# State-space outputs on two column tiles and the chunk kernel's product turned round on four

## The chip, the core and the metric

The kernel runs on one core of a Trainium2 chip. The metric is the time of one execution on the device in microseconds (us), and the median over several runs is compared.

## What is computed

A trunk of two layers over 256 tokens of 2048 channels. Layer 0 has a spatial-gating mixer, layer 1 a state-space mixer; a convolutional gated feed-forward follows each. The change touches the state-space mixer and what is prepared for it: 128 heads, each with 16 input channels, 64 complex states and 16 output channels.

```python
bbar_r, bbar_i = _cmul(qr[..., None], qi[..., None], b_re, b_im)      # per head: 64 states x 16 channels
def chunk_step(carry, u_c):
    bur = einsum('gpc,btgc->btgp', bbar_r, u_c); bui = ...            # inputs into the states
    pr, pim, hr, hi = associative_scan(combine, (a_r, a_i, bur, bui)) # h[t] = abar * h[t-1] + bu[t]
    ...
    y = einsum('gcp,btgp->btgc', cr, hr) - einsum('gcp,btgp->btgc', ci, hi) + dd * u_c
...
ga, gb = split(gelu(y) @ w_glu, 2); out = ga * sigmoid(gb)
```

Everything is float32.

## The kernel before

All large products run with weights streamed from HBM in tiles of up to 1 MB. `Weights` splits each tile into a high part (`wh`, L115, ScalarE) and a low part (`wl`, L116, VectorE), and `form_a_steps` multiplies blocks of 128 output features by 256 tokens: L767 is `wh` with 512 moving columns, L768 is `wl` with 256, into the tile `acc`. These two lines alternate through most of the kernel.

The state-space mixer works on chunks of 4 tokens. Its operators are built by `s5_prep` as background work: small steps of it are put between the weight tiles of layer 0's feed-forward. One of its parts, in the pool "prep_k", builds the chunk kernel, which leads from a chunk's inputs to its outputs, for 16 groups of 8 heads. Each group multiplies `qg` (128 states by 80 columns, stationary) with `bri` (128 states by 16 columns, moving) once per head, 8 float32 matmuls on L445 into `ps_k`. Each float32 matmul stands in the trace as two passes, so there are 16 records. ScalarE copies the 80 x 128 result (L449, `kc`), TensorE transposes it (L452, `ps_kt`), then VectorE (L454) and ScalarE (L460) place it in `tt`, and POOL's queue writes it to DRAM (L461, `td`). `bri` itself is filled earlier by four ScalarE copies (L386) with 16 columns per head.

In layer 1, `S5Tokens` handles 16 blocks of 8 heads (128 channels). Per block: `send` writes inputs u to DRAM, `load` reads them back (`ubd`) with the operator `pw`, `load1` reads tables, `load2` reads `qw` and `tw`, all on SP's queue; `drive` multiplies into `ps_x` (L574); `take`, `scan` and `turn` run the recurrence on VectorE and ScalarE; `outputs` makes `ps_y`; `gelu` applies the activation (L641, ScalarE) to `y` and writes it to DRAM (L642, SP's queue, `yd`); `fetch` reads it back turned (L646, POOL's queue, `yt`); `finish` splits it into `Gt` (L782, L783) for the gated product. The table `N_OF` puts each step in a slot between weight tiles; a scheduler then fixes the order on each queue. ScalarE, VectorE, SP and POOL each run in order, so a waiting instruction holds what is queued behind it. `ps_x` and `ps_y` share two PSUM buffers.

`outputs` has two sets of float32 matmuls with 64 output rows: L628, four on 128 moving columns (chunk inputs through `tw`, the chunk kernel), and L633, eight on 64 moving columns (states through `qw`, one per head). All go to PSUM partitions 0 to 63, 512 columns in all. `y` has one buffer.

Of the kernel before, what the change touches and what calls it, by code (L numbers as in the profile page):

```python
# [17 lines left out]
P = 128  # L18
# [17 lines left out]
def bcast(ap2d, n, axis):  # L36
    """[p, m] -> [p, n, m] (axis 1) or [p, m, n] (axis 2), repeated without a copy."""
    p, m = ap2d.shape
    if axis == 1:
        return ap2d.rearrange("p (o m) -> p o m", o=1).to_broadcast([p, n, m])  # L40
    return ap2d.rearrange("p (m o) -> p m o", o=1).to_broadcast([p, m, n])


def rsqrt_newton(nc, v, y, t):
    """y = v ** -0.5 (float32, three Newton steps); t is scratch."""
    V = nc.vector
    V.tensor_scalar(y.bitcast(I32), v.bitcast(I32), -0.5, RSQ, ALU.mult, ALU.add)
    for _ in range(3):
        V.scalar_tensor_tensor(t, y, -0.5, y, ALU.mult, ALU.mult)
        V.tensor_tensor(t, t, v, op=ALU.mult)  # L50
        V.scalar_tensor_tensor(y, t, 1.5, y, ALU.add, ALU.mult)


def rsqrt_column(nc, v, y, t, w):
    """rsqrt_newton for v of one column; t and w are scratch."""
    V = nc.vector
    V.tensor_scalar(y.bitcast(I32), v.bitcast(I32), -0.5, RSQ, ALU.mult, ALU.add)
    V.tensor_scalar(w, v, -0.5, None, ALU.mult)
    for _ in range(3):
        V.scalar_tensor_tensor(t, y, w, y, ALU.mult, ALU.mult)  # L60
        V.scalar_tensor_tensor(y, t, 1.5, y, ALU.add, ALU.mult)


# Slot of each group of 8 state-space heads, and how many slots later its results are read back and gated.
N_OF = (3, 4, 6, 7, 8, 9, 10, 11, 12, 13, 14, 16, 18, 20, 22, 24)
LAT = (4, 6)
# Products on constants that raise the tensor engine's clock while the input arrives.
N_WARM = 7
# Background work after each weight tile of the projection, of the FFN's up and of its down products.
# [5 lines left out]
class Weights:  # L75
    """Streams weight tiles in order of use and splits each into a high and a low float32r part."""
# [63 lines left out]
def w_tiles(w2d, k_chunk0, nk_total, col_segs, kt):  # L140
    """Tiles of a weight matrix: all of its K chunks for the given column segments."""
    out, k = [], 0
    width = sum(n for _, n in col_segs)
    while k < nk_total:
        nk = min(kt, nk_total - k)
        r0 = (k_chunk0 + k) * P
        segs = [
            (w2d[r0 : r0 + nk * P, c0 : c0 + n].rearrange("(k p) c -> p k c", p=P), n)
            for c0, n in col_segs
        ]  # L150
        out.append((segs, nk, width))
        k += nk
    return out


def exp_poly(nc, tl, x, out):
    """out = exp(x) in float32, by range reduction; tl(name, dtype) makes scratch like x."""
# [24 lines left out]
def sincos_poly(nc, tl, x, cos, sin):  # L182
    """cos and sin of x in float32, by reduction to a quarter turn."""
# [44 lines left out]
def s5_prep(tc, psum, ident, io, scr, rho):  # L228
    """Builds the state-space operators for chunks of 4 tokens and writes them to DRAM scratch.

    pd[h][c][j][(ri p)]   chunk input  -> state:  abar^(3-j) * Bbar
    qd[(ri p)][h][80]     state -> output: C * abar^tau (16 c x tau 1..4), then C itself
    td[(h % 2, c, j)][h // 2][(c' j')]  chunk input -> output inside the chunk, with the skip d on its diagonal
    rd[g][(h // 64, p)][2][16 h][64]  cos and sin of 4 * theta * k, heads 16 g .. of each half
    rho[(2 p), h]         |abar| ** 4

    Yields the vector engine's microseconds of each step, or None where the next step needs this one done.
    """
# [5 lines left out]
    with ExitStack() as keep:  # L244
        kp = keep.enter_context(tc.tile_pool(name="prep", bufs=1))
        tm = kp.tile([P, 512], F32, name="tm")
        bri = kp.tile([P, NH, 16], F32, name="bri")
# [3 lines left out]
        with ExitStack() as inner:  # L251
# [128 lines left out]
            for g in range(4):  # L380
                ps = psum.tile([P, 512], F32, name=f"ps_bri{g}", tag="misc")
                for i in range(4):
                    nc.tensor.transpose(
                        ps[:, i * P : (i + 1) * P], bb[:, 4 * g + i].rearrange("h r p -> h (r p)"), ident
                    )
                A.copy(  # L386
                    bri[:, :, 4 * g : 4 * g + 4].rearrange("q h c -> q c h"), ps.rearrange("q (c h) -> q c h", c=4)
                )
                yield 1.0
# [31 lines left out]
        with tc.tile_pool(name="prep_k", bufs=1) as pool:  # L421
# [17 lines left out]
            for g in range(16):  # L439
# [4 lines left out]
                for i in range(8):  # L444
                    nc.tensor.matmul(  # L445
                        ps[:80, i * 16 : (i + 1) * 16], qg[:, i, :], bri[:, 8 * g + i, :], start=True, stop=True
                    )
                kc = pool.tile([80, P], F32, name=f"kc{g}", tag="kc", bufs=2)
                A.copy(kc, ps[:80, :P])  # L449
                yield None  # L450
                ps = psum.tile([P, 512], F32, name=f"ps_kt{g}", tag="misc")
                nc.tensor.transpose(ps[:, :80], kc, ident[:80, :80])  # L452
# [54 lines left out]
class S5Tokens:  # L507
    """The state-space mixer for 8 heads (one block of 128 channels) at a time, in chunks of 4 tokens."""
# [21 lines left out]
    def send(self, s):  # L530
        """The block's inputs, to be read back as [(head, channel, token of chunk), chunk]."""
        ud = self.scr[4]
        self.nc.sync.dma_start(dram(ud, s * 32768, [[256, P], [1, 256]]), self.u.pop(s).rearrange("p j k -> p (j k)"))

    def load(self, s):
        """What the states need."""
# [12 lines left out]
    def load1(self, s):  # L549
        """What the scan needs."""  # L550
# [8 lines left out]
    def load2(self, s):  # L559
        """What the outputs need."""  # L560
# [8 lines left out]
    def drive(self, s):  # L569
        """Chunk inputs into the state space."""  # L570
# [7 lines left out]
    def take(self, s):  # L578
        """Into a frame that turns with the phase of abar ** 4."""
# [22 lines left out]
    def turn(self, s):  # L602
        """Back to the fixed frame; sp[.., h, k] is the state before chunk k."""
# [18 lines left out]
    def outputs(self, s):  # L622
        """States before each chunk and its inputs to y."""
# [3 lines left out]
        for i in range(4):  # L627
            nc.tensor.matmul(  # L628
                ps[:64, i * P : (i + 1) * P], st["tw"][:, i, :], st["ubd"][:, i, :],
                start=i == 0, stop=False, skip_group_check=True,  # L630
            )
        for h in range(8):
            nc.tensor.matmul(  # L633
                ps[:64, h * 64 : (h + 1) * 64], st["qw"][:, h, :64], st["sp"][:, h, :],
                start=False, stop=h == 7, skip_group_check=True,
            )

    def gelu(self, s):
        st = self.st.pop(s)
        y = self.pool.tile([64, 8, 64], F32, name=f"y{s}", tag="y", bufs=1)  # L640
        self.nc.scalar.activation(y.rearrange("q h k -> q (h k)"), st["y"][:64, :], AF.Gelu_apprx_tanh)  # L641
        self.nc.sync.dma_start(dram(self.scr[5], s * 32768, [[64, 64], [4096, 8], [1, 64]]), y)  # L642
# [11 lines left out]
def tile_hybrid_trunk(  # L654
# [86 lines left out]
    def bg(budget):  # L741
        """Runs steps of the background work for about that many microseconds of the vector engine."""
# [9 lines left out]
    def form_a_steps(Xt, nks, blocks, evac, k0=0):  # L752
        """Blocks of 128 output features by 256 tokens, weights stationary; yields after each weight tile.

        nks: chunks per weight tile, the first k0; blocks: column offset of each block in the tile; evac(pair, psum) follows
        each pair's last product.
        """
# [16 lines left out]
    def form_a(Xt, nks, blocks, evac, after=None, k0=0):  # L774
        """form_a_steps, with after[i]() behind tile i."""
# [4 lines left out]
    def split_to(dst, src):  # L780
        """dst[:, :256], dst[:, 256:] = high and low float32r parts of src."""
# [3 lines left out]
    def stage_x(k, g_col, src=None):  # L785
        """X[k] = parts of h[:, k] (or src) * g."""
# [7 lines left out]
    def sumsq(tp, k):  # L794
        """Adds the squares of h[:, k] to sq."""
# [7 lines left out]
    def make_r(tp):  # L803
        """rbc[:, t] = rsqrt(mean over channels of h ** 2 + eps), on every partition."""
# [9 lines left out]
    def residual(tp, ps, k, g_col=None, perm=False):  # L814
        """h[:, k:k+2] += product in ps; with g_col also the next stage's X and sum of squares."""
# [8 lines left out]
    def sum_parts(tp, ps, scaled=True):  # L824
        """(main + correction) [* r] of a pair of blocks -> [P, 2, 256] in SBUF."""
# [57 lines left out]
    def fetch_conv(tp, l):  # L883
        """Convolution taps and biases: loaded, then (place_conv) turned to a column per block of 128 channels."""
# [15 lines left out]
    def form_b_steps(Xt, nks, pss, own=0, between=None):  # L900
        """128 tokens by 512 output features in each of two banks, activations stationary; yields after each chunk.

        The last `own` chunks are taken by the first 128 tokens, then, after between(), by the others.
        """
# [25 lines left out]
    def total_r(ss, v, r, t):  # L930
        """r[:, a] = rsqrt(sum of ss[:, a, :] / D + eps)."""
# [10 lines left out]
    with ExitStack() as sgu_ctx:  # L942
# [33 lines left out]
        def turn_x(i):  # L976
            """Chunks 2 i and 2 i + 1 of the input, turned to channels by tokens."""
# [132 lines left out]
    n_tmp[0] = 1  # L1110
    with tc.tile_pool(name="s5", bufs=1) as sp:
# [58 lines left out]
        def glu_keep(i0):  # L1170
            """Half of the sum of a gate and value pair waits in the place of X."""
# [122 lines left out]
```

## Time and profile before

| | |
|---|---|
| runs of the kernel before | 2149.72 us median of three (2145.82 to 2150.45) |
| span of the profiled execution, first to last instruction | 2150.8 us |
| time of the profiled execution as a run | not listed apart; its span is 1.1 us above the median |
| TensorE busy | 2117.9 us, 98% of the span |
| VectorE, ScalarE busy | 1605.7 us, 1127.2 us |

A row of a timeline has the start in us, the duration in us, engine, line, operation, tiles and count; records that follow each other on one line are merged, and what stands in brackets is the idle time before them and what ended it. A matmul's duration runs to the end of its pipeline, so consecutive matmuls overlap, and the distance of their starts is what each costs. "128*64 128x128" is 128 rows by 64 columns of weights, and 128 rows by 128 columns of moving data. PE is TensorE, DVE VectorE, ACT ScalarE, and SPq the queue of SyncE that issues transfers.

### The profile page before, as it was taken

Reading aid. Unit: us, or ns where it says so; the run is one execution under the profiler, and the core shown is the slowest. Engines: PE = TensorE matmul, PEld = TensorE weight load, DVE = VectorE, ACT = ScalarE, POOL = GpSimd, SP = SyncE. Lnnn points to the kernel's source line nnn. Section 1 sums busy time; section 2 is a strip of 40 time slices with the busy share of each in tenths; the row PEclk is TensorE's granted clock in tenths of the full one; section 3 lists DMA queues with packets and bytes.
Section 4 is the critical chain, followed back from the end, with each engine's and each line's share of the span. In section 5 each row is a group of like instructions: output and inputs, shape, how many; then the busy total and the mean of one; then the engine's idle time right before and its main releaser. Section 6 shows DMA issues by size and latency. Waiting matters only on the chain.

```text
span 2150.8 us, 31583 instructions
## 1 busy us (share of the span) xinstructions
PE 2117.9 (98%) x12023; PEld 1829.1 (85%) x12023; DVE 1605.7 (75%) x2455; ACT 1127.2 (52%) x1682; POOL 90.2 (4%) x141
## 2 busy tenths in 40 slices
PE   8999999999999999999999999999999999999998
PEld 7888888888878888888888788888888888888886
DVE  6576788997997655899878866987665777557675
ACT  6544446553455534555556555555543555445553
POOL 1010000000002111000000000000000000000000
PEclk9999999999999999999999999999999999999999
DMA  7665556667668665665799986565565555655553
GB/s 259 196 187 171 192 188 203 219 213 232 208 208 253 211 203 179 193 214 188 246 277 272 254 236 190 184 204 183 181 205 183 181 193 183 198 191 178 194 196 117
DMA packets 359303, 438.84 MB, mean 204 GB/s; under 512 B 31376, under 2 KB 275696, under 8 KB 358512
## 3 DMA queue, kind: packets, MB, share of 16 engines
q1 hardware_dynamic: 349696, 407.94, 60.3%
q0 software_dynamic: 9424, 28.88, 4.4%
q8 instruction: 94, 1.54, 0.3%
q14 instruction: 57, 0.47, 0.1%
q10 hardware_dynamic: 32, 0.01, 0.0%
HBM read 414.66 MB, written 22.02 MB: 203 GB/s over the span
## 4 chain that ended last, share of the span: by engine, by line
PE 88%; DMA 5%; DVE 4%; issue 1%; ACT 1%; SPq 0%; ACTq 0%; DVEq 0%
PE acc L767 47%; PE acc L768 24%; PE accb L911 4%; PE accb L910 4%; PE accb L912 4%; PE accv L911 1%; PE accv L912 1%; PE accv L910 1%; DMA yd<-y 1%; DVE wl L116 1%; DMA w<-in_b_w_glu_dram 1%; PE ps_k L445 1%; DMA vn<-in_x_dram 1%; DMA w<-in_b_w_in_dram 0%; PE ps_x L574 0%
## 5 line engine op out<-in xcount | busy, mean ns | idle before, releaser
L767 PE MATMUL acc<-X,wh 128*128 128x512 f32 x3328 | 1174.8, 398 | 1.3 <-DVE z L829 0.8
L116 DVE TENSOR_TENSOR wl<-w,wh 128x1024 fp32r<-128x1024 f32 (+1 forms) x721 | 867.3, 1219 | 394.7 <-ACT wh L115 390.2
L115 ACT CAST wh<-w 128x1024 fp32r<-128x1024 f32 (+1 forms) x721 | 735.9, 1047 | 707.2 <-PE acc L767 525.5
L768 PE MATMUL acc<-X,wl 128*128 128x256 f32 x3328 | 930.6, 281 | 2.5 <-DVE wl L116 2.5
L767 PEld LDWEIGHTS acc<-X,wh 128*128 128x128 f32 x3328 | 623.2, 188 | 148.5 <-DVE z L829 1.7
L768 PEld LDWEIGHTS acc<-X,wl 128*128 128x128 f32 x3328 | 628.3, 189 | 6.7 <-DVE wl L116 3.9
L767 PE MATMUL acc<-Gt,wh 128*128 128x512 f32 x1472 | 519.2, 398 | 0.8 <-DVE kept L1177 0.8
L768 PE MATMUL acc<-Gt,wl 128*128 128x256 f32 x1472 | 409.2, 281 | 0.0
L767 PEld LDWEIGHTS acc<-Gt,wh 128*128 128x128 f32 x1472 | 275.2, 188 | 64.6 <-DVE kept L1177 1.2
L768 PEld LDWEIGHTS acc<-Gt,wl 128*128 128x128 f32 x1472 | 278.0, 189 | 2.4
L910 PE MATMUL accb<-wh,Gt 128*128 128x512 f32 x352 | 136.8, 389 | 0.0
L912 PE MATMUL accb<-wh,Gt 128*128 128x512 f32 x352 | 136.8, 389 | 0.0
L911 PE MATMUL accb<-wl,Gt 128*128 128x512 f32 x352 | 136.8, 389 | 0.0
L845 ACT ACTIVATE a<-z,conv 128x256 f32<-128x256 f32 x176 | 96.2, 595 | 17.1 <-DVE z L831 16.9
L827 ACT COPY t<-acc 128x512 f32<-128x512 f32 x96 | 55.7, 580 | 75.0 <-PE acc L768 75.0
L829 DVE TENSOR_TENSOR z<-acc,t 128x512 f32<-128x512 f32 x96 | 65.8, 685 | 25.5 <-ACT t L827 25.3
L851 DVE SCALAR_TENSOR_TENSOR a<-z,conv,a 128x254 f32<-128x254 f32 x176 | 80.3, 475 | 0.0
L848 DVE SCALAR_TENSOR_TENSOR a<-z,conv,a 128x255 f32<-128x255 f32 x176 | 77.3, 476 | 1.0 <-ACT a L845 1.0
L910 PEld LDWEIGHTS accb<-wh,Gt 128*128 128x128 f32 x352 | 66.1, 188 | 13.9
L912 PEld LDWEIGHTS accb<-wh,Gt 128*128 128x128 f32 x352 | 66.1, 188 | 13.8
L911 PEld LDWEIGHTS accb<-wl,Gt 128*128 128x128 f32 x352 | 66.1, 188 | 13.5
L831 DVE TENSOR_TENSOR z<-z,rbc 128x512 f32<-128x512 f32 x96 | 65.8, 686 | 1.2
(303 smaller groups left out, 1394.7 us busy)
## 6 DMA issues: line engine op xcount, KB each, us to landing
w<-in_f_w_up_dram SPq DMA_DIRECT2D x352, 512.0 KB, 4.6
w<-in_f_w_down_dram SPq DMA_DIRECT2D x80, 1024.0 KB, 5.1
w<-in_a_w_in_dram SPq DMA_DIRECT2D x31, 1024.0 KB, 5.6
w<-in_b_w_glu_dram SPq DMA_DIRECT2D x62, 512.0 KB, 5.3
w<-in_a_w_out_dram SPq DMA_DIRECT2D x16, 1024.0 KB, 5.0
w<-in_b_w_in_dram SPq DMA_DIRECT2D x16, 1024.0 KB, 8.3
w<-in_f_w_down_dram SPq DMA_DIRECT2D x16, 512.0 KB, 3.7
tab<-rd SPq DMA_DIRECT2D x32, 256.0 KB, 7.2
```

The costliest lines, as they stand in the source:

```text
L115: self.nc.scalar.copy(hi[:, a:b], raw[:, o + a : o + b])
L116: self.nc.vector.tensor_tensor(lo[:, a:b], raw[:, o + a : o + b], hi[:, a:b].bitcast(F32), op=ALU.subtract)
L767: T.matmul(ps, wh, Xt[k], start=k == k_first, stop=False, skip_group_check=True)
L768: T.matmul(ps[:, NT:], wl, Xt[k][:, :NT], start=False, stop=k == ktot - 1, skip_group_check=True)
L829: V.tensor_tensor(z, ps[:, :, :NT], t, op=ALU.add)
L831: V.tensor_tensor(z, z, rb2, op=ALU.mult)
L845: A.activation(a[:, q], z[:, q], AF.Identity, bias=cw[:, 3, c : c + 1], scale=cw[:, 2, c : c + 1])
L848: V.scalar_tensor_tensor(a[:, q, 1:], z[:, q, : NT - 1], cw[:, 1, c : c + 1], a[:, q, 1:], ALU.mult, ALU.add)
L851: V.scalar_tensor_tensor(a[:, q, 2:], z[:, q, : NT - 2], cw[:, 0, c : c + 1], a[:, q, 2:], ALU.mult, ALU.add)
L910: T.matmul(pss[tt], xh, w[0], start=k == 0, stop=False)
L911: T.matmul(pss[tt], xh, w[1], start=False, stop=False)
L912: T.matmul(pss[tt], xl, w[0], start=False, stop=k == ktot - 1)
```

## The change

In `outputs`, heads 0 to 3 go to PSUM partitions 0 to 63 and heads 4 to 7 to partitions 64 to 127, 256 columns each, with `tile_position` (0, 0) and (0, 64), and consecutive matmuls alternate between the two. `y` becomes 128 x 4 x 64 with two buffers, GELU reads 128 x 256, and two writes of 64 partitions each replace the one of 512 columns.

The chunk kernel's product is turned round: `bri` is now the stationary operand and `qg` the moving one, and two heads share 32 output rows. `bri` has 48 columns for each pair of heads, the middle 16 zero, so that columns 0 to 31 are the even head and zeros and columns 16 to 47 zeros and the odd head. Four pairs go to four tiles of 32 columns. The result comes out as the transpose gave it, so the copy `kc` and the transpose go.

```diff
-        bri = kp.tile([P, NH, 16], F32, name="bri")
+        bri = kp.tile([P, NH // 2, 48], F32, name="bri")
+        nc.gpsimd.memset(bri[:, :, 16:32], 0.0)
...
-                A.copy(
-                    bri[:, :, 4 * g : 4 * g + 4].rearrange("q h c -> q c h"), ps.rearrange("q (c h) -> q c h", c=4)
-                )
+                for e in range(2):
+                    A.copy(
+                        bri[:, :, 32 * e + 4 * g : 32 * e + 4 * g + 4].rearrange("q m c -> q c m"),
+                        ps.rearrange("q (c m e) -> q c m e", c=4, e=2)[:, :, :, e],
+                    )
...
-                for i in range(8):
-                    nc.tensor.matmul(
-                        ps[:80, i * 16 : (i + 1) * 16], qg[:, i, :], bri[:, 8 * g + i, :], start=True, stop=True
-                    )
-                kc = pool.tile([80, P], F32, name=f"kc{g}", tag="kc", bufs=2)
-                A.copy(kc, ps[:80, :P])
+                for e in range(2):
+                    for j in range(4):
+                        nc.tensor.matmul(
+                            ps[32 * j : 32 * j + 32, :80], bri[:, 4 * g + j, 16 * e : 16 * e + 32], qg[:, 2 * j + e, :],
+                            start=e == 0, stop=e == 1, skip_group_check=True, tile_position=(0, 32 * j),
+                        )
                 yield None
-                ps = psum.tile([P, 512], F32, name=f"ps_kt{g}", tag="misc")
-                nc.tensor.transpose(ps[:, :80], kc, ident[:80, :80])
...
-        for i in range(4):
+        for i in (0, 2, 1, 3):
+            o = 64 * (i // 2)
             nc.tensor.matmul(
-                ps[:64, i * P : (i + 1) * P], st["tw"][:, i, :], st["ubd"][:, i, :],
-                start=i == 0, stop=False, skip_group_check=True,
+                ps[o : o + 64, i % 2 * P : i % 2 * P + P], st["tw"][:, i, :], st["ubd"][:, i, :],
+                start=i % 2 == 0, stop=False, skip_group_check=True, tile_position=(0, o),
             )
-        for h in range(8):
+        for h in (0, 4, 1, 5, 2, 6, 3, 7):
+            o = 64 * (h // 4)
             nc.tensor.matmul(
-                ps[:64, h * 64 : (h + 1) * 64], st["qw"][:, h, :64], st["sp"][:, h, :],
-                start=False, stop=h == 7, skip_group_check=True,
+                ps[o : o + 64, h % 4 * 64 : h % 4 * 64 + 64], st["qw"][:, h, :64], st["sp"][:, h, :],
+                start=False, stop=h % 4 == 3, skip_group_check=True, tile_position=(0, o),
             )
...
-        y = self.pool.tile([64, 8, 64], F32, name=f"y{s}", tag="y", bufs=1)
-        self.nc.scalar.activation(y.rearrange("q h k -> q (h k)"), st["y"][:64, :], AF.Gelu_apprx_tanh)
-        self.nc.sync.dma_start(dram(self.scr[5], s * 32768, [[64, 64], [4096, 8], [1, 64]]), y)
+        y = self.pool.tile([P, 4, 64], F32, name=f"y{s}", tag="y", bufs=2)
+        self.nc.scalar.activation(y.rearrange("q h k -> q (h k)"), st["y"][:, :256], AF.Gelu_apprx_tanh)
+        for i in range(2):
+            self.nc.sync.dma_start(
+                dram(self.scr[5], s * 32768 + i * 16384, [[64, 64], [4096, 4], [1, 64]]), y[64 * i : 64 * i + 64]
+            )
```

## Rows read from the trace of the kernel before

**Rows 1.** The page: span, busy time of each engine, the chain that ended last

```profile
span 2150.8 us, 31583 instructions
PE 2117.9 (98%) x12023; PEld 1829.1 (85%) x12023; DVE 1605.7 (75%) x2455; ACT 1127.2 (52%) x1682; POOL 90.2 (4%) x141
...
PE 88%; DMA 5%; DVE 4%; issue 1%; ACT 1%; SPq 0%; ACTq 0%; DVEq 0%
```

**Rows 2.** Stretches: length, PE, PEld, DVE, ACT, POOL busy, PEclk, DMA share, GB/s

```profile
660.00:865.00 205.00, 205.00 (x1329) 181.70 (x1329) 126.12 (x174) 96.36 (x192) 32.65 (x32) 1.00 0.68 208
1110.00:1240.00 130.00, 121.20 (x860) 104.06 (x861) 108.21 (x146) 80.16 (x120) 6.78 (x12) 1.00 1.07 266
1240.00:1250.00 10.00, 7.76 (x39) 6.77 (x38) 8.74 (x13) 8.12 (x13) 0.54 (x1) 0.83 1.09 272
1250.00:1300.00 50.00, 50.00 (x324) 43.60 (x323) 31.75 (x39) 27.72 (x39) 2.69 (x5) 1.00 0.66 204
```

**Rows 3.** TensorE in order of time, one chunk-kernel product

```profile
689.64 0.28 PE L768 MATMUL acc<-X,wl 128*128 128x256 f32 x1
689.76 1.25 PE L445 MATMUL ps_k<-bri,qg 128*80 128x16 f32 x16
690.87 0.48 PE L767 MATMUL acc<-X,wh 128*128 128x512 f32 x1
691.18 0.28 PE L768 MATMUL acc<-X,wl 128*128 128x256 f32 x1
```

**Rows 4.** The same view, one transpose

```profile
696.16 0.39 PE L767 MATMUL acc<-X,wh 128*128 128x512 f32 x1
696.39 0.29 PE L768 MATMUL acc<-X,wl 128*128 128x256 f32 x1
696.51 0.23 PE L452 MATMUL ps_kt<-ident,kc 80*128 80x80 f32 x1
696.54 0.48 PE L767 MATMUL acc<-X,wh 128*128 128x512 f32 x1
696.86 0.28 PE L768 MATMUL acc<-X,wl 128*128 128x256 f32 x1
```

**Rows 5.** Groups of instructions by shape, 660 to 865 us; busy us, mean ns

```profile
L449 ACT COPY kc<-ps_k 80x128 f32<-80x128 f32 x16 | 4.1, 258 | 0.9 <-PE ps_k L445 0.9
```

**Rows 6.** TensorE in order of time, the last output block

```profile
1279.52 0.28 PE L768 MATMUL acc<-Gt,wl 128*128 128x256 f32 x1
1279.73 1.09 PE L628 MATMUL ps_y<-ubd,tw 128*64 128x128 f32 x8
1280.65 1.09 PE L633 MATMUL ps_y<-sp,qw 128*64 128x64 f32 x16
1281.67 0.50 PE L767 MATMUL acc<-Gt,wh 128*128 128x512 f32 x1
1282.01 0.28 PE L768 MATMUL acc<-Gt,wl 128*128 128x256 f32 x1
```

**Rows 7.** The same view, cut to six passes

```profile
1279.99 0.82 PE L628 MATMUL ps_y<-ubd,tw 128*64 128x128 f32 x6
```

**Rows 8.** Groups of instructions by shape, 1060 to 1300 us; behind the second bar, waits

```profile
L574 PE MATMUL ps_x<-ubd,pw 128*128 128x128 f32 x128 | 19.1, 293 | 9.4 <-ACT y L641 3.9 <-DMA ubd<-ud 1.7 <-DVE q L600 1.3
L628 PE MATMUL ps_y<-ubd,tw 128*64 128x128 f32 x128 | 17.4, 279 | 2.6 <-DVE q L599 1.4 <-ACT y L641 1.1
L641 ACT ACTIVATE y<-ps_y 64x512 f32<-64x512 f32 x16 | 9.4, 591 | 13.6 <-DMA yd<-y 12.7 <-PE ps_y L633 0.9
L782 ACT CAST Gt<-yt 128x256 fp32r<-128x256 f32 x16 | 6.5, 406 | 32.9 <-DMA yt<-yd 32.8
```

**Rows 9.** TensorE in order of time, a product at the lower clock

```profile
1243.93 2.08 PE L574 MATMUL ps_x<-ubd,pw 128*128 128x128 f32 x8 [2.23 <-ACT y L641]
```

**Rows 10.** Instructions of line 642; min/median/max ns, first and last start

```profile
L642 SPq DMA_DIRECT2D yd<-y x16: 580/604/1074, 1123.4 to 1285.4; - x16
```

**Rows 11.** SP's waits from 1095 to 1300 us: total, times, longest

```profile
SPq L99 <- DVE wl L116: 34.2, 11, 7.7
```

## Prediction, made before the change was run

> **What bounds the kernel now.** I read the page first: the span is 2150.8 us, TensorE is busy for 98% of it and holds 88% of the chain that ended last [rows 1]. So a piece that TensorE no longer runs is a gain wherever TensorE has no idle time. The second view is busy time by stretch [rows 2]. While the chunk kernel is built (660 to 865 us, beside the feed-forward of layer 0) TensorE is busy 205.00 of 205.00 us, VectorE 126, ScalarE 96, and the DMA share is 0.68: TensorE alone sets the time, and each us cut from it counts in full. The state-space mixer (1100 to 1300 us) is two stretches. From 1110 to 1250 us the DMA share is 1.07 to 1.09, and TensorE still loses time: busy 121.20 of 130 us and 7.76 of 10, so 11.0 us idle. From 1250 us on the DMA share is 0.66 and TensorE is busy 50.00 of 50 [rows 2]. Of the 16 blocks' output products, thirteen lie before 1250 us, where transfers and TensorE end together, and three behind it, where TensorE alone counts (the last one is [rows 6]).
>
> **The switch of tile width, which the trace shows already.** Around an output block [rows 6] the last full product starts at 1279.52 and the first product on 64 columns at 1279.73: 0.21 us, where a product of L768 is followed after 0.12 us otherwise [rows 3, 4]. The block takes 1279.73 to 1281.67 = 1.94 us. The next full product takes 0.34 us to its follower, instead of 0.23 [rows 4]. Every float32 matmul is two passes: six passes on 128 moving columns take (0.82 - 0.28) / 5 = 0.109 us each, the last one's own 0.28 taken off [rows 7, 8]; the sixteen on 64 columns take 1.02 with the way out, which I set equal to the 0.09 of the way in, so 0.058 each. Passes alone are 8 x 0.109 + 16 x 0.058 = 1.80 us; the rest of the excursion, 0.09 before + 0.14 inside + 0.11 behind, is 0.34 us of switching. The chunk kernel's product on 80 columns shows no such gap: it starts 0.12 us after a full product [rows 3].
> The Trainium skill (TensorEngine Tiling (Array Packing), Tiling Modes) has the rule: changing the tiling mode, not just the tile, drains the engine; this speaks against moving an 80-column product to 32-column tiles, and the rows agree with 0.09 us on either side of a 64-column block and none at 80. Without any switching the sum below would be 16 x 0.34 = 5.4 us lower.
>
> **Chunk kernel, removed.** Per group of 8 heads, sixteen passes from 689.76 to 690.87 = 1.11 us, and 0.08 behind them (0.31 to the next product for 0.23) [rows 3, 4]; the transpose 0.03 and 0.09 behind it [rows 4]. That is 1.31 us x 16 groups = 21.0 us of TensorE (sixteen copies of the results, [rows 5]). The ScalarE copy between them, 16 x 0.258 = 4.1 us [rows 5], was covered by TensorE and gains nothing.
>
> **Chunk kernel, added.** Again sixteen passes (8 matmuls), but with 32 weight columns (half of them zeros) and 80 moving ones. Moving: between 0.058 at 64 and 0.109 at 128 columns, 0.071 is my estimate for 80. Weights: 80 columns with only 16 moving ones step at 1.11 / 16 = 0.07 us, so 0.9 ns a column and 0.03 us for 32: moving columns bind. Every group now makes an excursion to another tile width: 0.34 us, from the 64-column row. What the trace does not show is whether passes on different column tiles run side by side. The bounds:
> - no overlap: 16 x 0.071 + 0.34 = 1.48 us, 0.17 more than before, +2.7 us in all;
> - only weight loads bind: 16 x 0.03 + 0.07 + 0.34 = 0.89, 0.42 less, -6.7 us;
> - between: the two passes of one matmul sit in one tile and follow each other, but the first pass of the next matmul, in the next tile, starts with the second pass of this one. Then 9 pass times, 0.64 + 0.34 = 0.98 us, 0.33 less, **-5.3 us**. I take this one: program order puts both passes of a matmul together, and the rows show matmuls starting in that order.
> The stretch has TensorE at 205 of 205 us, and the next engine, VectorE, at 126: nothing hides or limits this.
>
> **Outputs.** The 64-column width was there before, so no switch is added. The passes now alternate between two column tiles. No overlap: 0. If the matmuls overlap but weight loads come one after another (24 x 0.058): 1.39 for 1.80, -0.41 us a block. If loads overlap as well, in the order above: 4 x 0.109 + 8 x 0.058 + 0.058 = 0.96, -0.84. I take -0.41, since the rows show weight loads on one path only. For the three blocks behind 1250 us: -1.2 us (bounds 0 and -2.5). For the thirteen before it TensorE's saving runs into transfers that stay the same in bytes; I count none of it.
>
> **The buffer of y.** y goes from one buffer to two of half the width. GELU, with ScalarE stopped behind it, waited 12.7 us for y's own write, and TensorE waited for GELU: 3.9 + 1.1 = 5.0 us [rows 8]. These waits go. Next in line are the transfers (DMA share 1.07) and ScalarE's wait for y's return, yt, 32.8 us [rows 8], both untouched. So between 0 and -5.0; I take half, **-2.5**. GELU itself shortens from 0.591 us [rows 8], off the path. In 1240 to 1250 us the granted clock is 0.83 on average [rows 2]: for a few us it stood at the lower of its two levels, 1.2 GHz, behind a TensorE wait of 2.23 us, and eight passes of 128 moving columns took 2.08 us, for 7 x 0.109 + 0.28 = 1.04 [rows 7, 9]. Whether this recurs is a toss; with the full products behind it I put it at 1.7 us either way, kept for the range.
>
> **Edits at no cost.** y leaves in two writes instead of one: 16 more issues of 0.604 us on SP [rows 10] = 9.7 us, in front of weight loads, tw and ubd. SP waits 34.2 us there for weight buffers to come free (11 times) [rows 11], which covers them; uncovered they would cost up to 9.7. POOL's fetch of y, alone on its queue here, waits for both. Bytes and piece size are unchanged. The four copies to bri become eight of half the size on ScalarE (busy 52% of the span), and the memset goes to POOL (4%), both long before the first product [rows 1].
>
> **Sum.** -5.3 - 1.2 - 2.5 = -9.0 us. Against the profiled span 2150.8 that is 2141.8; the median of the runs is 1.1 lower than the span, so **2140.7 us**.
>
> **The rivals.**
> 1. *Nothing overlaps* (the change doesn't do what it says): +2.7 in the chunk kernel, 0 in the outputs, about -1 from y: 2151.4 us, within 0.2%. For it: no row shows two passes side by side; steps are 0.058 and 0.11 throughout. Against: in these rows every pass uses the same columns.
> 2. *Full overlap*: -6.7, three blocks at half of 1.80, -2.7, y's waits all gone, -5.0: 2135.3 us. The Trainium skill (TensorE: Matmul & The Clock Gate, Part 3) tells of three 32-column tiles that ran 2.38 times as fast together; no run here shows it, and its matmuls are not float32 pairs.
> 3. *Slower: every change of tile empties the array*, not only a change of width. Price 0.09 us a change, as in [rows 6]; place: 7 changes in each chunk product and 11 in each output block. Chunk kernel: 16 x (0.17 + 7 x 0.09) = +12.8; three output blocks 3 x 11 x 0.09 = +3.0; together about 2165.5 us, more if the thirteen blocks count. It decides from 11 ns a change: 2.7 + (112 + 33) x 0.011 = 4.3. Against: 24 passes, each with its own weights, show no such gap inside the block of [rows 6], but they never leave one tile.
> 4. *The DMA-bound stretch decides otherwise*: the extra issues on SP push weight loads, up to +9.7, or the stretch shrinks by all of its 11.0 us of idle time.
>
> **How the numbers follow.** Chances: forecast 0.52, rival 1 0.20, rival 2 0.10, rival 3 0.10, rival 4 0.08. A measurement of this kernel tells about 0.2% (4.3 us) from no change, so "faster" starts below 2145.4. The forecast's own range, 2134 to 2147, is faster nine times in ten; rival 2 always, rival 4 half, rival 1 seldom: 0.62. Same: most of rival 1, the rest of the forecast: 0.24. Slower: rival 3, a little of 1 and 4: 0.14. Range: from 2132 (rival 2 with the clock's 1.7 and a little more of the stretch) to 2153 (rival 1 with nothing from y and another us); it leaves out rival 3 and the far ends of 4.
>
> **What would show it.** In the chunk kernel: starts of passes closer than 0.07 us, product and switching together near 0.98 us a group, no transpose; 1.48 would be rival 1, above 2 rival 3. In the outputs: a block from its first pass to the next full product near 1.5 us for 1.94. GELU no longer waiting for yd, and idle TensorE between 1110 and 1250 us down from 11.0 us. The forecast is wrong if the passes keep their steps, or if the mixer's idle time grows by what its products give back.

## The result and the profile after

The changed kernel takes 2135.41 us (median of four runs, 2133.26 to 2137.83); the kernel before, beside it on the same chip, 2150.09 us (2145.82 to 2152.34). The ratio is 0.9946, 95% interval 0.9931 to 0.9961, so about 11.6 us less. The forecast was 2140.7 us, with a range of 2132 to 2153. The profiled execution took 2135.51 us as a run; its span is 2133.8 us, 17.0 below that of [rows 1]. About 3 us of these 17 arose before the end of weight split 12 (splits are counted from 0), where the change has no part yet: this kernel reached it after 38.6 us and the one before after 41.6, and the kernels of experiments 1 to 5, which are alike up to there, after 38.5 to 40.4. That is why the ratio is the size of the effect, and why the stages below are compared one by one.

The page of the changed kernel (span, busy time of each engine, chain that ended last):

```profile
span 2133.8 us, 31582 instructions
PE 2098.5 (98%) x12007; PEld 1803.1 (85%) x12007; DVE 1604.1 (75%) x2455; ACT 1122.0 (53%) x1670; POOL 91.3 (4%) x142
...
PE 89%; DMA 5%; DVE 4%; issue 1%; SPq 1%; ACT 0%; POOL 0%; ACTq 0%; DVEq 0%; POOLq 0%
```

Against [rows 1] there are 16 matmul records fewer, the transposes. The kernel is bound as before: TensorE 98%, and nearly nine tenths of the chain.

**The chunk kernel.** TensorE of the changed kernel in order of time, the product that answers to [rows 3]; then the same view cut off before 684.49 us, where three of its passes had started:

```profile
684.03 0.40 PE L773 MATMUL acc<-X,wh 128*128 128x512 f32 x1
684.27 0.28 PE L774 MATMUL acc<-X,wl 128*128 128x256 f32 x1
684.48 0.48 PE L449 MATMUL ps_k<-qg,bri 128*32 128x80 f32 x16
684.89 0.50 PE L773 MATMUL acc<-X,wh 128*128 128x512 f32 x1
685.22 0.28 PE L774 MATMUL acc<-X,wl 128*128 128x256 f32 x1
```

```profile
684.48 0.27 PE L449 MATMUL ps_k<-qg,bri 128*32 128x80 f32 x3
```

Sixteen passes take 684.48 to 684.89 = 0.41 us, for 1.11 in [rows 3]. Entry takes 0.21 instead of 0.12, and the next full product 0.33 to its follower instead of 0.23: 0.09 + 0.41 + 0.10 = 0.60 us a group, for 1.31 with the transpose. One such pass lasts 0.257 us, and three of them end 0.27 after the first one's start, so they start 7 ns apart: passes on different column tiles do run side by side.

**The output block** that answers to [rows 6], the same view:

```profile
1263.93 0.28 PE L774 MATMUL acc<-Gt,wl 128*128 128x256 f32 x1
1264.14 0.66 PE L630 MATMUL ps_y<-ubd,tw 128*64 128x128 f32 x8
1264.62 0.64 PE L636 MATMUL ps_y<-sp,qw 128*64 128x64 f32 x16
1265.19 0.50 PE L773 MATMUL acc<-Gt,wh 128*128 128x512 f32 x1
1265.52 0.28 PE L774 MATMUL acc<-Gt,wl 128*128 128x256 f32 x1
```

1264.14 to 1265.19 is 1.05 us for 1.94: 0.89 less in a block, 14.2 us for the sixteen. Entry (0.21) and the product behind it (0.33) are what they were.

**The mixer did not keep all of that.** Stretches of the changed kernel that answer to [rows 2] (length, busy time of PE, PEld, DVE, ACT, POOL, granted clock, DMA share, GB/s):

```profile
650.00:860.00 210.00, 209.36 (x1390) 178.15 (x1389) 134.97 (x189) 102.19 (x187) 34.89 (x39) 1.00 0.73 220
1110.00:1240.00 130.00, 116.51 (x883) 97.56 (x882) 109.32 (x151) 81.69 (x127) 7.89 (x14) 0.93 1.06 281
1250.00:1300.00 50.00, 50.00 (x319) 43.26 (x318) 30.39 (x36) 24.38 (x33) 1.08 (x2) 1.00 0.65 202
```

The first and the last are bound by TensorE alone, as before. In the middle one TensorE is idle for 13.5 us; before, 1110 to 1250 us had 11.0. The mean granted clock there is 0.93 for 1.00.

To compare stages whose start has moved, the ends of certain weight splits on VectorE serve as landmarks: split 216 to 360 of the 721 holds the chunk kernel, 360 to 432 the mixer.

| us | before | changed | changed, taken again |
|---|---|---|---|
| chunk kernel stage | 422.7 | 415.8 | 415.8 |
| mixer | 267.4 | 260.8 | 262.9 |
| what follows | 806.8 | 806.1 | 806.8 |

So the chunk kernel's stage gave 6.9 us and the mixer 4.5 to 6.6 of 14.2. The mixer from end to end, the kernel before and then the changed one (columns as above):

```profile
1056.00:1323.50 267.50, 254.69 (x1659) 220.12 (x1658) 205.73 (x274) 153.82 (x222) 13.85 (x26) 0.99 0.94 256
```

```profile
1046.00:1306.80 260.80, 245.28 (x1659) 209.81 (x1658) 204.95 (x274) 150.69 (x222) 13.90 (x26) 0.96 0.94 263
```

TensorE's busy time fell by 9.4 us, not by 14.2, and its idle time rose from 12.8 to 15.5: 9.4 - 2.7 = 6.7 us kept. The 4.8 between 14.2 and 9.4 is not measured apart. Two things go that way: the order of the steps moved a little, which gives 26 excursions to the other width for 23 (by the prediction's price 3 x 0.34 = 1.0 us), and TensorE is busy for 13.5 us at half the clock, for 3.2 before (as an estimate, half of the difference, 5.2 us, would go at the full clock). Together these estimates come to more than the 4.8.

### The profile page after: what moved, and what is told of

Read it like the earlier page. It is cut to its first block, busy times and chain, and to the rows that moved or that the text cites. A ratio compares the mean times of both kernels' runs of the same rounds, so it can differ in the third digit from the quotient of the medians.

```text
span 2133.8 us, 31582 instructions
## 1 busy us (share of the span) xinstructions
PE 2098.5 (98%) x12007; PEld 1803.1 (85%) x12007; DVE 1604.1 (75%) x2455; ACT 1122.0 (53%) x1670; POOL 91.3 (4%) x142
## 4 chain that ended last, share of the span: by engine, by line
PE 89%; DMA 5%; DVE 4%; issue 1%; SPq 1%; ACT 0%; POOL 0%; ACTq 0%; DVEq 0%; POOLq 0%
PE acc L773 48%; PE acc L774 24%; PE accb L918 4%; PE accb L917 4%; PE accb L916 4%; DVE wl L116 1%; PE accv L917 1%; PE accv L918 1%; PE accv L916 1%; DMA w<-in_b_w_in_dram 1%; DMA qd<-qt 1%; DMA vn<-in_x_dram 1%; DMA pw<-pd 1%; PE ps_x L575 1%; DMA ud<-u 0%
```

## Experiments

**1. Each part alone.** The first kernel is the changed one with `outputs` and `gelu` as before; the second is the kernel before with the new `outputs` and `gelu`, and the old chunk kernel.

```diff
# e_chunk, against the changed kernel
-        y = self.pool.tile([P, 4, 64], F32, name=f"y{s}", tag="y", bufs=2)
+        y = self.pool.tile([64, 8, 64], F32, name=f"y{s}", tag="y", bufs=1)
...
# e_outs, against the kernel before: the other way round
```

> The chunk kernel's product turned round on four column tiles, alone; outputs and y as in the kernel before. Theory: products on different tiles run fully side by side, so each of the 16 groups costs 0.72 to 0.8 us instead of 1.31 on a TensorE that is never idle there: about -7 us, 2143 us. Rival (the gain is the mixer's, and the chunk kernel only moves idle time): within 2 us of before.

> Outputs on two column tiles and y in two buffers, alone; the chunk kernel as before. Theory: TensorE saves 0.89 us x 16 = 14 us, but thirteen blocks lie in the stretch where transfers are full, so about half is kept: -7 us, 2143 us, and idle TensorE in that stretch larger than before. Rival (TensorE alone sets the mixer's time): -14 us, 2136 us. Rival (transfers alone set it): -2.7 us, 2147 us, the last three blocks only.

The chunk part alone: 2140.37 us for 2146.16, ratio 0.9972 [0.9959, 0.9986], -6.0 us. Its stage takes 415.8 us, as with the whole change, and its mixer 267.6, as before: the part is worth what its stage shows. The outputs alone: 2145.26 us, 0.9993 [0.9983, 1.0002], -1.5 us, with 263.4 us for its mixer, 4.0 less than before. So this part gives 1.5 to 4 us of the 14.2 that its products save. That is less than the 7 expected, and nearest to the 2.7 of the rival in which transfers alone set the mixer's time; the interval of the run does not exclude no change.

**2. Program order of the tiles.** Matmuls of one tile next to each other; all else as in the changed kernel.

```diff
-                for e in range(2):
-                    for j in range(4):
+                for j in range(4):
+                    for e in range(2):
...
-        for i in (0, 2, 1, 3):
+        for i in range(4):
...
-        for h in (0, 4, 1, 5, 2, 6, 3, 7):
+        for h in range(8):
```

> The changed kernel with matmuls of one tile issued next to each other: chunk kernel pair by pair (both heads of a tile, then the next tile), outputs heads 0 to 7 in order. Theory (the engine starts passes in program order, so alternation is what makes them overlap): chunk product 13 pass times of 0.071 + 0.34 = 1.26 us instead of about 0.75, +8 us, outputs 7 x 0.109 + 15 x 0.058 = 1.63 instead of 0.9, +2 us or more: 2145 to 2150 us. Rival (the engine picks waiting passes of other tiles by itself): steps as in the changed kernel, 2135 us.

2138.65 us, 0.9963 [0.9951, 0.9975]: by the ratios 1.3 to 3.6 us slower than the changed kernel in its two sets of runs (0.9957 and 0.9946; the intervals overlap), and still faster than before. The theory asked for 2145 to 2150. TensorE of this kernel in order of time, one chunk product and one output block; then the first cut off before 683.42 us:

```profile
683.16 0.28 PE L774 MATMUL acc<-X,wl 128*128 128x256 f32 x1
683.37 0.51 PE L449 MATMUL ps_k<-qg,bri 128*32 128x80 f32 x16
683.80 0.50 PE L773 MATMUL acc<-X,wh 128*128 128x512 f32 x1
...
1266.58 0.28 PE L774 MATMUL acc<-Gt,wl 128*128 128x256 f32 x1
1266.79 0.67 PE L630 MATMUL ps_y<-ubd,tw 128*64 128x128 f32 x8
1267.27 0.92 PE L636 MATMUL ps_y<-sp,qw 128*64 128x64 f32 x16
1268.12 0.50 PE L773 MATMUL acc<-Gt,wh 128*128 128x512 f32 x1
```

```profile
683.37 0.30 PE L449 MATMUL ps_k<-qg,bri 128*32 128x80 f32 x4
```

With four passes in a row on one tile, the chunk product takes 0.43 us for 0.41, and four passes start within 0.30 - 0.257 = 0.04 us. They are 14 ns apart instead of 7, so the new order did reach the engine. The rows do not name the column tile of a pass. But strictly in program order a tile could only begin with the last of the four passes of the tile before it, 13 pass times or some 0.9 us in all by the prediction's 0.071 a pass. So TensorE starts passes of other tiles while earlier ones wait. That has an end: the products through `tw`, with four passes in a row on a tile, keep their time (0.48 us); those through `qw`, with eight in a row, take 0.85 us for 0.57, still under the 1.02 of one tile. The Trainium skill (TensorE: Matmul & The Clock Gate, Part 3) says that matmuls start strictly in order; for these float32 passes the measurement shows otherwise.

**3. One buffer for y.**

```diff
-        y = self.pool.tile([P, 4, 64], F32, name=f"y{s}", tag="y", bufs=2)
+        y = self.pool.tile([P, 4, 64], F32, name=f"y{s}", tag="y", bufs=1)
```

> The changed kernel with one buffer for y instead of two. Theory: GELU again waits for y's own writes (12.7 us of ScalarE before) and TensorE behind it: +2 to +5 us, 2138 to 2140 us. Rival (transfers set the stretch anyway): waits return, time the same within 2 us.

2150.47 us, 1.0025 [1.0014, 1.0036], with 279.0 us for the mixer, 18 more, and further off than either expectation. GELU waits for `yd` again, and TensorE behind it (engine, tile, line, what released it, us in total, times, longest):

```profile
ACT y L644 <- DMA yd<-y: 20.5, 7, 6.1
PE ps_x L575 <- ACT y L644: 10.3, 2, 7.9
```

With another 2.6 us before L630, TensorE waits 12.9 us for GELU here and 4.3 in the changed kernel. This looks like a high value of the second buffer, but the scheduler made another order on TensorE, VectorE, ScalarE and SP out of this one edit, so the run does not part the buffer from the order. Experiment 6 tries to.

**4. Fewer transfers in the mixer.** The tables `tab` are loaded for the first three blocks alone and used again by the others, in the kernel before (`e_notab_b`) and in the changed one (`e_notab_a`). These kernels leave out 26 transfers, 6.8 MB; their recurrence turns by the wrong angles from the fourth block on.

```diff
-        tab = self.pool.tile([P, 2, 512], F32, name=f"tab{s}", tag="tab", bufs=3)
+        if s >= 3:
+            self.st[s]["tab"] = self.tabs[s % 3]
+            return
+        tab = self.pool.tile([P, 2, 512], F32, name=f"tab{s}", tag=f"tab{s}", bufs=1)
+        self.tabs = getattr(self, "tabs", []) + [tab]
```

> The kernel before, with the scan's tables (tab, 512 KB a block) loaded for the first three blocks alone; the other thirteen reuse them, so this part of the data is wrong in meaning and its loading is left out: 6.8 MB and 26 issues fewer on SP in the mixer. Theory (transfers fill the stretch from 1110 to 1250 us): TensorE's 11 us of idle time go for the most part: 2136 to 2140 us. Rival (the chain of in-order waits through y sets it): half of that, 2141 us or more.

> The changed kernel, its tables loaded for the first three blocks alone, as in e_notab_b. Theory: with transfers relieved the mixer keeps all of the 14 us that TensorE saves there, plus 7 in the chunk kernel: 20 to 21 us under e_notab_b, hardly any time at the lower clock. Rival (what is given back comes from ScalarE's and SP's order, not from bytes): 12 to 14 us under e_notab_b, as the change is against the kernel before.

2136.52 us (0.9950 [0.9933, 0.9966]), as the theory expected, and 2124.82 us (0.9898 [0.9883, 0.9913]): with lighter transfers the change is worth 11.7 us, about what it is worth with all of them, and not the 20 that the theory of a DMA-bound mixer asked for. In both kernels the scheduler moved other work as well, some of SP's other transfers among it, so lighter transfers and a new order are not parted here either. Their mixers from end to end, first without and then with the change:

```profile
1053.00:1310.30 257.30, 254.34 (x1658) 220.03 (x1657) 204.42 (x274) 152.94 (x221) 13.89 (x26) 0.99 0.81 240
```

```profile
1048.10:1298.50 250.40, 243.21 (x1659) 206.81 (x1658) 203.50 (x273) 150.00 (x222) 13.89 (x26) 0.99 0.85 246
```

Without the change and with a DMA share of 0.81, TensorE is nearly without idle time (257.3 - 254.3 = 3.0 us for 12.8): with the transfers of the tables, most of that waiting went, and 10 us of the kernel's time. With the change TensorE saves 11.1 us of busy time and its idle time rises from 3.0 to 7.2, 4.0 of which is one wait for GELU to free PSUM. It keeps 6.9. So waits come back even where the transfers have room.

**5. Another queue for y, other slots for the outputs.** `e_actq` issues the writes of y from ScalarE's queue; `e_spread` spreads the outputs of the last eight blocks over later weight tiles.

```diff
# e_actq
-            self.nc.sync.dma_start(
+            self.nc.scalar.dma_start(
# e_spread
-N_OF = (3, 4, 6, 7, 8, 9, 10, 11, 12, 13, 14, 16, 18, 20, 22, 24)
+N_OF = (3, 4, 6, 7, 8, 9, 10, 11, 13, 15, 16, 18, 20, 22, 24, 26)
```

> The changed kernel with y's two writes issued from ScalarE's queue instead of SP's. Theory (transfers set the stretch): same within 2 us as the changed kernel. Rival (SP's queue, with 16 more issues of 0.6 us and waits for GELU in front of the weight loads, sets it): 3 to 9 us less than the changed kernel, less idle TensorE in the stretch.

> The changed kernel with blocks 8 to 15 spread over later slots (13, 15, 16, 18, 20, 22, 24, 26 instead of 12, 13, 14, 16, 18, 20, 22, 24). Theory: fewer bytes a slot where transfers are full, so less idle TensorE and less time at the lower clock: 3 to 8 us less than the changed kernel. Rival (the stretch is decided by the first eight blocks, which are not moved): same within 2 us.

2149.53 us, 1.0023 [1.0012, 1.0034], and 2141.62 us, 0.9981 [0.9971, 0.9991]: both slower than the changed kernel, which none of the expectations named, with mixers of 275.1 and 270.6 us and TensorE idle for 27 and 23 of them. The waits are new ones: 10.1 us for a state of the recurrence (`q`) in the first, 10.3 us for `qw` in the second. In both the scheduler changed the order of the other work too, so neither tells what SP's 16 further issues cost. That stays open.

**6. The scheduler's search for an order turned off,** so that one edit moves less of the rest. `p_b` is the kernel before so, `p_a` the changed one, `p_y1` the changed one with one buffer for y. SP and POOL then have the same order in all three. TensorE does not: some products of `drive` and `outputs` stand elsewhere among the full products, and between `p_b` and `p_a` some steps on VectorE and ScalarE moved as well.

```diff
-    with _tile.TileContext(nc, schedule_with_timeline_sim=True) as tc:
+    with _tile.TileContext(nc, schedule_with_timeline_sim=False) as tc:
```

> The kernel before, its instructions ordered without the planner's simulated timeline (one switch in the launch code). In this form the queues of SP and POOL stand in the same order with the change and without it, and VectorE's nearly so. This run is the base for p_a and p_y1; its own time may lie 10 us on either side of the kernel before.

> The changed kernel, ordered without the simulated timeline, SP's and POOL's order as in p_b. Theory (what the mixer gives back in the changed kernel comes from the new order that the planner made for it): the mixer keeps 12 to 14 us and the chunk kernel 7, so 18 to 21 us under p_b. Rival (the mixer is bound by transfers, and TensorE's savings turn into waits under any order): 7 to 13 us under p_b, idle TensorE in the mixer 5 us or more above p_b's.

> As p_a, with one buffer for y instead of two, order on SP and POOL as in p_a. Theory (the 18 us that e_y1 lost in the mixer came for the most part from the order that the planner made for it): within 4 us of p_a. Rival (the second buffer is worth that much by itself): 10 us or more above p_a.

> The changed kernel once more, on the chip and beside the runs of the experiments, as a reference for them: 0.993 to 0.996 of the kernel before, mixer 260 to 263 us as in its first trace. If its mixer comes out above 266 us, the differences seen between the experiments there are scatter between executions and not their edits.

2182.28, 2179.97 and 2182.41 us (1.0163 [1.0148, 1.0178], 1.0152 [1.0137, 1.0167], 1.0166 [1.0151, 1.0182]); the changed kernel again, beside them, 2138.04 us, 0.9957 [0.9940, 0.9973], with 262.9 us for its mixer as expected. In this order the change is worth 2.3 us, less than either expectation for `p_a`, and the two intervals overlap. By the landmarks it is 6.0 less in the chunk kernel's stage and 2.6 more in the mixer. The mixers, before and changed:

```profile
1067.20:1359.30 292.10, 267.87 (x1676) 230.44 (x1675) 206.36 (x274) 153.99 (x223) 13.87 (x26) 0.95 0.85 235
```

```profile
1060.90:1355.60 294.70, 257.29 (x1676) 218.93 (x1675) 206.71 (x273) 150.77 (x223) 13.85 (x26) 0.94 0.83 233
```

TensorE saves 10.6 us of work and waits 13.2 us more (24.2 to 37.4 us of idle time). What it waits for (engine, tile, line, what released it, us in total, times, longest), of the kernel before and the changed one in this order:

```profile
PE acc L768 <- DVE wl L116: 13.9, 11, 2.8
PE ps_y L628 <- ACT wh L115: 7.3, 3, 4.0
PE acc L767 <- ACT wh L115: 1.7, 2, 1.0
```

```profile
PE acc L774 <- DVE wl L116: 25.5, 15, 4.2
PE acc L773 <- ACT wh L115: 9.6, 5, 2.9
```

Waits for the splitting of a weight tile grew from 22.9 us to 35.1. This fits shorter products that bring TensorE to the next weight tile before it is ready; as TensorE's own order moved too, it is not shown to be the only reason.

One y buffer instead of two (`p_y1`) leaves the mixer at 292.1 us, 2.6 under `p_a`, and the kernel 2.4 us above it, within what the intervals allow. But in this order GELU has no wait for `yd` at all, in `p_b` or in `p_y1`, both with one buffer, where it waited 12.7 us in the kernel before. So the run says nothing of the buffer's worth in an order that has this wait, and how the 18 us of experiment 3 divide between the buffer and the new order stays open.

## Why the prediction was right, and where it was not

**What bounds the kernel: right.** What the chunk kernel's stage saved came out as time, with the change alone as with the whole (415.8 us in both, experiment 1), the mixer kept less than half of its saving, and the rest of the kernel stood still.

**Chunk kernel, size 5.3 us: 6.9 in its stage, 6.0 by the runs of that part alone. Right in sign, the group's price wrong.** The step that failed is "the first pass of the next matmul, in the next tile, starts with the second pass of this one", taken because "program order puts both passes of a matmul together". Nine pass times, 0.98 us a group, were forecast; 0.60 were measured. Experiment 2 shows that program order does not bind the passes. The price of a change of width held nearly: 0.34 was forecast, and four pass times of 0.071, one tile's share, leave 0.32 of the 0.60. The rule that a change of tiling mode drains the engine (the Trainium skill, TensorEngine Tiling (Array Packing), Tiling Modes) agrees with the 0.09 that the entry now costs at the turned product. The prediction's "none at 80" holds for the way in alone: behind the old 80-column product the next full product took 0.08 more as well [rows 3], so the 0.10 behind the new one is not a price of the width alone.

Rival 2's -6.7 for this part lies near the measured -6.9, but not for its reason, which was 0.89 us a group. Taken from the starts of all 2301 full products and 16 groups in the stage, the groups cost 20.6 us before (21.0 in the prediction) and 10.3 now (0.7 of it a wait for `qg`): 10.3 less. The full products took 402.0 us before and take 405.5 now. **3.5 us of the gain were given back by unchanged instructions.** TensorE in order of time in the same part of the stage, ten pairs of full products of the kernel before and then of the changed one:

```profile
890.24 0.39 PE L767 MATMUL acc<-X,wh 128*128 128x512 f32 x1
890.47 0.28 PE L768 MATMUL acc<-X,wl 128*128 128x256 f32 x1
...
893.70 0.39 PE L767 MATMUL acc<-X,wh 128*128 128x512 f32 x1
893.93 0.28 PE L768 MATMUL acc<-X,wl 128*128 128x256 f32 x1
```

```profile
880.02 0.40 PE L773 MATMUL acc<-X,wh 128*128 128x512 f32 x1
880.25 0.28 PE L774 MATMUL acc<-X,wl 128*128 128x256 f32 x1
...
883.55 0.40 PE L773 MATMUL acc<-X,wh 128*128 128x512 f32 x1
883.79 0.28 PE L774 MATMUL acc<-X,wl 128*128 128x256 f32 x1
```

Ten pairs take 3.46 us there and 3.53 here, at a granted clock of 1.00 in both. From split 240 to 312 the mean pair, taken by 24 splits at a time, takes 353.2 to 353.6 ns in the ten kernels that have the turned product, and 346.6 to 351.9 in the four that do not (the kernel before, `e_outs`, `e_notab_b`, `p_b`). That the turned product causes the slower rhythm is not shown. The last of these products starts at 838.4 us, so the rows of the changed kernel above lie 42 us behind it. Both rhythms occur elsewhere in both kernels, and the kernel before has the slower one, 353.3 ns, from 800 to 840 us among its old products. What sets the rhythm is open, and no run was made for it.

**Outputs: price of a block wrong, sum nearly right.** -0.41 us a block was taken ("the rows show weight loads on one path only"); -0.89 was measured, so loads of two tiles overlap as well: the far bound, -0.84, was the right one. For the three blocks behind 1250 us that is -2.7 instead of -1.2. "I count none" of the thirteen before came near, but its reason is not borne out: transfers were said to hold that stretch, and with lighter transfers (and another order) no more of the gain is kept (experiment 4).

**The buffer of y: GELU's wait went, TensorE's did not.** Groups of the changed kernel's mixer that answer to [rows 8] (count, busy us, mean ns, idle time before them and what ended it):

```profile
L630 PE MATMUL ps_y<-ubd,tw 128*64 128x128 f32 x128 | 11.0, 294 | 4.9 <-ACT y L644 4.3 <-DMA tw<-td 0.6
L575 PE MATMUL ps_x<-ubd,pw 128*128 128x128 f32 x128 | 20.5, 312 | 5.4 <-DMA ubd<-ud 2.0 <-DMA yd<-y 2.0 <-DMA pw<-pd 1.1
L644 ACT ACTIVATE y<-ps_y 128x256 f32<-128x256 f32 x16 | 6.1, 381 | 2.0 <-PE ps_y L636 1.9
L788 ACT CAST Gt<-yt 128x256 fp32r<-128x256 f32 x16 | 6.5, 405 | 22.5 <-DMA yt<-yd 22.4
```

GELU no longer waits for yd (12.7 us before), as forecast. TensorE still waits 4.3 us for GELU, for 5.0 before. The longest of these waits, 3.41 us, ends at 1195.18 us. GELU stands there on ScalarE behind a wait of 6.23 us for the recurrence's `q` (ScalarE in order of time):

```profile
1192.26 0.62 ACT L611 COPY rs<-q 64x512 f32<-64x512 f32 x1 [6.23 <-DVE q L601]
...
1194.74 0.38 ACT L644 ACTIVATE y<-ps_y 128x256 f32<-128x256 f32 x1
```

So "these waits go" failed for TensorE; what the buffer is worth by itself stays open (experiments 3 and 6). The -2.5 counted for it and the -1.2 of the outputs make -3.7 for the mixer; it gave -4.5 to -6.6. The whole stood near, -9.0 for some -11.6, because the prices of the chunk product and of the block were too cautious while the wait that the -2.5 came from stayed. That much of the agreement is luck.

**The lower clock: forecast as a toss of 1.7 us, it recurred and grew.** The changed kernel, TensorE in order of time, three records that follow each other, with the idle time before them in brackets:

```profile
1191.09 0.69 PE L636 MATMUL ps_y<-sp,qw 128*64 128x64 f32 x16 [1.92 <-DVE sp L616]
1195.18 1.12 PE L630 MATMUL ps_y<-ubd,tw 128*64 128x128 f32 x8 [3.41 <-ACT y L644]
1199.53 0.80 PE L773 MATMUL acc<-Gt,wh 128*128 128x512 f32 x1 [3.23 <-DVE Gt L789]
```

and two stretches at the lower clock, columns as in the others:

```profile
1168.70:1172.10 3.40, 3.40 (x16) 3.11 (x15) 2.96 (x5) 1.17 (x2) 0.54 (x1) 0.50 1.02 278
1192.60:1206.20 13.60, 6.70 (x39) 5.26 (x40) 7.56 (x12) 6.59 (x13) 0.54 (x1) 0.50 1.08 268
```

At 0.50 the clock is at its lower level, 1.2 GHz. It fell at 1192.6 us, in the second of these waits, which follows the first after one product, and stood there for 13.6 us; in the whole mixer it was there for 20.5 us, for 3.4 before. The product through `tw` takes 1.12 us there for 0.66 in the output block above. So such waits can cost twice: their own length, and the slower work behind them.

**Idle TensorE down from 11.0 us: wrong.** It went up (13.5 us in 1110 to 1240). The prediction named this as a sign that it would be wrong: "if the mixer's idle time grows by what its products give back". It grew by a part, 2.7 us, under the scheduler's order, and by 13.2 with its search turned off. Which waits take the place depends on the order; that some do was seen in both.

**The issues on SP** were put at nothing; no run isolates them.

## What to carry to other kernels

Small float32 matmuls gain much from column tiles: an output block took 1.05 us for 1.94 on two, the chunk product 0.41 for 1.11 on four. With four passes in a row on a tile the order of issue made hardly any difference; with eight it took back 0.28 of the 0.45 us that the products through `qw` had gained. But the kernel keeps the gain best where TensorE alone sets the time: the same kind of edit gave 6.9 of 10.3 us in a stage without idle time, and 4.5 to 6.6 of 14.2 in one with waits. Price each change of tile width (0.34 us here), and look at the unchanged products beside it, too. Where a scheduler orders the work, an edit of one buffer can come with another order of everything else (experiment 3, the mixer 18 us longer). So hold the order fixed to measure a part, and look first whether that order has the wait which the part removes (in experiment 6 it had not).

## What the runs showed of the hardware

- Passes of four column tiles start 7 ns apart, and 16 float32 passes with 32 weight columns and 80 moving ones take 0.41 us, for 1.11 of the product before it was turned round (80 weight columns, 16 moving, one tile); the two passes of a float32 matmul hold back nothing on the other tiles.
- TensorE starts passes of other tiles ahead of waiting ones: order made 0.02 us of difference at four passes in a row on a tile, and 0.28 us at eight.
- Full products alternate at 346 or at 353 ns a pair, at the same granted clock, for stretches of 70 us and more; what sets which is open.
- Behind two waits of TensorE, 1.92 and 3.41 us with one product between, the granted clock was at 1.2 GHz for 13.6 us.
